# Second layer's chosen tokens: gathered rows and transposes in place of one-hot products

## The chip, the cores and the metric

The kernel runs on one core of a Trainium2 chip, with all weights and inputs in that chip's memory. The metric is the device time of one execution in microseconds, here the median of three runs.

## What is computed

Two layers of a backbone over 512 latent tokens and 256 context tokens of 1024 features, float32. Each layer mixes the tokens (an mLSTM in both directions, a convolution, a Fourier transform, one projection in and one out) and then sends them through 16 experts that choose their own tokens. Only the second part matters here; of the reference it is this (`cap` is 64 for the latents, 32 for the context):

```python
def expert_choice_ffn(xn, w_router, w_gate, w_up, w_down):
    bsz, n, _ = xn.shape
    cap = EC_CAPACITY_FACTOR * n // N_EXPERTS
    aff = jax.nn.softmax(jnp.einsum('bnd,de->bne', xn, w_router).astype(jnp.float32), axis=-1)
    gate, idx = lax.top_k(jnp.swapaxes(aff, 1, 2), cap)
    bidx = jnp.arange(bsz)[:, None, None]
    xs = xn[bidx, idx]
    hid = jax.nn.silu(jnp.einsum('becd,edf->becf', xs, w_gate)) * jnp.einsum('becd,edf->becf', xs, w_up)
    ys = jnp.einsum('becf,efd->becd', hid, w_down) * gate[..., None].astype(xn.dtype)
    return jnp.zeros_like(xn).at[bidx, idx].add(ys)
```

The second layer's experts see the latents alone, since nothing reads the context after it. A final norm over the latents follows.

## The kernel before, in words

**Experts.** They go in pairs, one on each half of the partitions: 8 pairs, each with a gate, an up and a down product of 64 slots by 1024 by 1024 per expert. `wide` (line 1397) does one such product in four quarters; a quarter (q) takes two weight tiles, one of each expert, and issues eight products of 512 columns (line 1410; each is two instructions of the trace). Between the quarters it fills in small work: `pop(turns)` the next pair's tokens, `pop(scat)` the sums into the stream (line 1476), `pop(trans)` the transposes of the hidden values (line 1463). The order on PE is the program's (`manual_schedule`); the other engines' order is set by a scheduler. The loop at line 1646 does gate(p+1), down(p), up(p+1); the last pair's down product, `down_last`, goes by quarters of the columns (line 1618), and the squares for the final norm ride along.

**Weights.** `load_experts` (line 1123) issues the loads on SP's queue in the order in which they are used, one tile of 1 MiB (two blocks of 128 rows of one expert) at a time, into a ring of places `wreg`; a tile that has been used gives its place back. In the second layer the ring has 9 places of its own, filled while the output projection runs, 6 more (`WP`) once the projection's operands are gone, and 1 (`extra`, line 1300): 16. Each load of the ring takes one of eight semaphores in turn.

**The chosen tokens.** After the second norm DVE picks each expert's best tokens by eight rounds of max, index and replace (lines 1234 to 1240), while PE turns the normalised latents into rows by token, `XT`, which ACT copies out of PSUM (lines 1254 and 1255). The places are turned into columns by slot: `GI` and `GP` hold them as floats, `GXu` as whole numbers.

- In the *first layer* the token rows are written to `xrow` in memory by SP (line 1257); `fetch_rows` (line 1332) lets POOL gather a pair's 128 rows by an indirect DMA (line 1337), and `turn` turns them to features by slots with four transposes for each half of the features (line 1363).
- In the *second layer* the rows stay in the buffer. `onehot` (line 1341) spreads a pair's places by one product and compares them on DVE with the token numbers `tcol` (line 1347); `turn` then makes the features by slots with 16 products for each half (line 1360).

In both, DVE and ACT scale and shift the result into `XSp` (lines 1368 and 1370). `fetch_pair(q)` puts a pair's turns on the list, two pairs ahead of their use for the gathers, and the lists are emptied between the quarters. At the stage's start the second layer does the one-hot and the first half's turn before the first gate product, and the second half's turn after that product's first quarter (line 1638):

```python
if last:
    wreg.append(extra)
    load_experts()
fetch_pair(0)
pop(turns, 2 if last else 99)
if not last:
    wreg += wp[4:] + xt_r + [mem.alloc(2048) for _ in range(3)]
    load_experts(gathers)
```

Of the kernel before, what the change touches and what calls it, by code (L numbers as in the profile page):

```python
# [10 lines left out]
OP = mybir.AluOpType  # L11
# [3 lines left out]
D = 1024  # L15
KB = 8
# [6 lines left out]
LAT, CTX = 0, 1  # L23
# [26 lines left out]
ADA1_RATE, AREG, ADA_XTK = 0.3, 19, 1.2  # L50
WORDER = [[KB0 + i for i in range(4)] + p + [QB + i for i in range(4)] + [FB, FB + 1] + [OB + i for i in range(4)]
# [7 lines left out]
class Mem:  # L59
    """Places in the on-chip buffer, in floats of a partition."""  # L60
# [45 lines left out]
class Fill:  # L106
    """Work that is laid between the steps of another: rate is its share of their time."""
# [18 lines left out]
    def run_us(self, us):  # L126
        """about us of it, now"""
        self.credit = us / self.rate * self.rate
        self.run(0.0)
# [25 lines left out]
def build(nc, tc, xT, ctxT, params, w_ada, w_gates, w_in, w_out, w_router, w_e_gate, w_e_up, w_e_down,  # L155
# [6 lines left out]
    def body(A, RB, PS, scr, xrow):  # L162
# [30 lines left out]
        # the float32r operands live in tiles of their own; the place of the largest one is  # L193
        # given to expert weights while no projection runs
# [17 lines left out]
        # ------------------------------------------------------------ constants  # L212
# [7 lines left out]
        _, tcol = new(4)  # L220
# [23 lines left out]
        pool.iota(tcol, pattern=[[128, 4]], base=0, channel_multiplier=1, allow_small_or_imprecise_dtypes=True)  # L244
# [15 lines left out]
        # silu(c), silu(c_ctx) as the two used columns of a 32-column stationary  # L260
# [3 lines left out]
        # ------------------------------------------------------------ adaLN vectors  # L264
        def after(inst, firsts, how=mybir.DependencyClass.Sync):
            """a transfer that takes its turn after others"""
            for f in firsts:
                tc.add_manual_dep(inst.ins, f.ins.name, mybir.DependencyInfo(how, mybir.DependencyReason.DATA),
                                  reason="its turn comes later")

        def ada_round(l, r, ring, bank, eng, firsts=(), some=1):
            ps = B(bank)
            src = w_ada[l].rearrange("(k p) (r g h c) -> r h k p g c", p=128, r=3, g=4, h=2)
            for hf in range(2):
                for k in range(KB):
# [5 lines left out]
                    # some at a time: the array's tiling changes as seldom as it can  # L281
# [14 lines left out]
        def ada_first(ring, bank, bank2, eng, splits):  # L296
            """the first layer's first vectors, by halves of the columns: blocks 0, 1, 4, 5 of the features first"""
# [3 lines left out]
            for hf in range(2):  # L301
# [8 lines left out]
                # the first weights' splits come before  # L310
# [19 lines left out]
        # ------------------------------------------------------------ norms  # L330
        class Sums:
            """sums of squares over the features: four blocks at a time, each on its group of partitions"""
# [16 lines left out]
            def columns(self, out, sb, ps, eng):  # L349
                """1 / root mean square, by token: out [128, chunks]"""  # L350
# [8 lines left out]
        def warm(func, after):  # L359
            """have the function's table in place, after the making of a column, before it is waited for"""  # L360
# [6 lines left out]
        def spread(cols, nch, tmp, ps):  # L367
            """values by token [128, chunks] as rows on every partition"""
# [22 lines left out]
        # ================================================================ a layer  # L391
        for l in range(2):
# [5 lines left out]
            # ---------------- projection weights: loads and splits run ahead of the products  # L398
# [13 lines left out]
            def split_ahead(n):  # L412
                while len(parts) < min(n, len(wseq)):
# [4 lines left out]
                    # the vector engine is the busier one while the convolution runs  # L418
# [13 lines left out]
            # ---------------- first vectors, norm  # L432
# [74 lines left out]
            def gate_rows(some, half):  # L507
                # the gates: four blocks at a time, each on its group of partitions
# [5 lines left out]
            # the first layer's by blocks, while the second half of the vectors comes; the second's  # L514
            # context first, as its sums end before
# [48 lines left out]
            def in_block(label, which):  # L564
# [4 lines left out]
                # the last product leaves the blocks in the order in which the next one's operands take their place  # L569
# [6 lines left out]
            def tview(ap, h, s):  # L576
                """[p, 512] in the head's own token order, seen in raster order [p, r, w]."""
# [9 lines left out]
            # gates: rows 32*(2*dir + head//2) + head%2 (i) and + 2 (f)  # L587
# [41 lines left out]
            def chain():  # L629
                # the gate rows  # L630
# [37 lines left out]
                # the backward scan of the context starts at its last chunk, from nothing  # L668
# [21 lines left out]
                # by tokens: column 4*dir + head  # L690
# [9 lines left out]
                # the running maxima and the states' weights go out, and come back on every partition  # L700
# [3 lines left out]
                # decay, on every partition  # L704
# [17 lines left out]
                # chunk states  # L722
# [40 lines left out]
                def fetch(h):  # L763
                    """a head's rows of both directions on every partition; what a query may not see is masked"""
# [10 lines left out]
                def front(s, h):  # L775
                    """scores of a head, weighted for both directions; queries weighted for the states"""
# [74 lines left out]
                # normalise, transpose, gate; the result takes the gate's place  # L851
# [67 lines left out]
            def convln():  # L919
# [6 lines left out]
                # convolution: LayerNorm, swish  # L926
# [52 lines left out]
            for part in (('v', 'ga') if l == 0 and not GA0 else ('ga', 'v')):  # L979
                if part == 'ga':  # L980
# [16 lines left out]
                    # convolution: the sums take the gates' place  # L997
# [37 lines left out]
            # ---------------- Fourier input, folded: the transform of real numbers  # L1035
# [53 lines left out]
            # ---------------- the output projection; the second norm's sums and the router ride along  # L1089
# [24 lines left out]
            # expert weights run ahead from here on  # L1114
# [8 lines left out]
            def load_experts(firsts=(), most=1000):  # L1123
                while len(wtiles) < min(wtaken[0] + len(wreg), len(wq), most):
                    w, e, i = wq[len(wtiles)]
                    if last and w is w_e_down and e >= E - 2:
                        t = V(wreg[len(wtiles) % len(wreg)], KB, 256)
                        src = w[l, e].rearrange("(k p) f -> p k f", p=128)[:, :, i * 256:i * 256 + 256]
                        # the very last ones in halves: fewer products wait for the end of the transfer
# [632 lines left out]
```

## Time and profile before

| | us |
|---|---|
| runs | 1888.52, 1891.25, 1892.82 |
| median | 1891.25 |
| span of the profiled execution | 1887.4 |
| PE, DVE, ACT, POOL busy in it | 1777.9, 688.1, 452.6, 128.1 |

The profile comes from one execution of its own; only its span is given, from the first to the last instruction, and it lies 1.1 us below the fastest of the three runs. A busy PE is not a PE at its peak, and the shares are means over stages with different limits: the first layer's expert stage lies at about 470 to 1000 us, the second layer's at about 1394 to 1870 us. 518.40 MB are moved in all, most of them the 2 x 192 expert tiles. A row of the stretches gives each engine's busy time with the number of instructions, TensorE's granted clock as a share of full speed, the mean busy share of the 16 DMA engines, and the rate.

### The profile page before, as it was taken

Reading aid. Unit: us, or ns where it says so; the run is one execution under the profiler, and the core shown is the slowest. Engines: PE = TensorE matmul, PEld = TensorE weight load, DVE = VectorE, ACT = ScalarE, POOL = GpSimd, SP = SyncE. Lnnn points to the kernel's source line nnn. Section 1 sums busy time; section 2 is a strip of 40 time slices with the busy share of each in tenths; the row PEclk is TensorE's granted clock in tenths of the full one; section 3 lists DMA queues with packets and bytes.
Section 4 is the critical chain, followed back from the end, with each engine's and each line's share of the span. In section 5 each row is a group of like instructions: output and inputs, shape, how many; then the busy total and the mean of one; then the engine's idle time right before and its main releaser. Section 6 shows DMA issues by size and latency. Waiting matters only on the chain.

```text
span 1887.4 us, 25008 instructions
## 1 busy us (share of the span) xinstructions
PE 1777.9 (94%) x10336; PEld 970.1 (51%) x10336; DVE 688.1 (36%) x1490; ACT 452.6 (24%) x868; POOL 128.1 (7%) x164
## 2 busy tenths in 40 slices
PE   5989999998999999999999998989979999999997
PEld 2667887776333333333333477777744444334433
DVE  4533897424002212122122577956230222111213
ACT  4433454313111001101100363346221101000001
POOL 1022221321000000000000002210000000000000
PEclk8989999998999999999999999999989999999999
DMA  9365344855999999988988113143669999999993
GB/s 340 101 201 194 99 134 148 293 207 218 415 414 384 352 343 345 354 340 325 353 327 320 40 34 95 56 121 101 238 253 416 416 414 414 415 416 416 416 396 120
DMA packets 151377, 518.40 MB, mean 275 GB/s; under 512 B 9696, under 2 KB 29152, under 8 KB 151264
## 3 DMA queue, kind: packets, MB, share of 16 engines
q1 hardware_dynamic: 135392, 456.51, 63.1%
q0 software_dynamic: 15872, 60.30, 9.6%
q8 instruction: 81, 1.33, 0.3%
q14 instruction: 32, 0.26, 0.0%
HBM read 509.96 MB, written 6.82 MB: 274 GB/s over the span
## 4 chain that ended last, share of the span: by engine, by line
PE 76%; DVE 10%; DMA 5%; issue 5%; ACT 2%; SPq 1%; POOL 1%; DVEq 0%; POOLq 0%; ACTq 0%
PE PS L1410 31%; PE PS L485 16%; PE PS L1420 9%; PE PS L1360 3%; PE PS L1476 3%; DVE A L1010 2%; DMA A<-w_e_up 2%; PE PS L279 1%; PE PS L1618 1%; SPq L304 1%; DVE A L1477 1%; PE PS L1497 1%; DMA WP<-w_e_up 1%; PE PS L1463 1%; DMA A<-w_e_down 1%
## 5 line engine op out<-in xcount | busy, mean ns | idle before, releaser
L485 PE MATMUL PS<-RA,RB 128*128 128x512 f32 (+1 forms) x2352 | 513.1, 365 | 19.0 <-ACT A L968 8.0
L1410 PE MATMUL PS<-A 128*64 128x512 f32 x1600 | 427.5, 596 | 5.1 <-DMA A<-w_e_up 4.4
L485 PEld LDWEIGHTS PS<-RA,RB 128*128 128x128 f32 x2352 | 376.9, 193 | 93.8 <-issue 20.8
L1410 PE MATMUL PS<-WP,A 128*64 128x512 f32 x1344 | 370.4, 597 | 1.4 <-DMA WP<-w_e_up 1.4
L1410 PEld LDWEIGHTS PS<-A 128*64 128x64 f32 x1600 | 130.7, 137 | 223.0 <-issue 206.5
L1410 PEld LDWEIGHTS PS<-WP,A 128*64 128x64 f32 x1344 | 111.8, 137 | 180.0 <-issue 173.0
L1477 DVE SCALAR_TENSOR_TENSOR A<-PS,A 128x512 f32<-128x512 f32 x128 | 91.9, 748 | 228.3 <-PE PS L1476 228.3
L1464 ACT ACTIVATE A<-PS 128x512 f32<-128x512 f32 x40 | 23.8, 597 | 354.9 <-PE PS L1463 354.8
L1420 PE MATMUL PS<-WP,A 128*32 128x512 f32 x816 | 108.7, 595 | 0.0
L1010 DVE SCALAR_TENSOR_TENSOR A<-A 128x783 f32<-128x783 f32 (+1 forms) x120 | 107.5, 922 | 0.1
L1368 ACT ACTIVATE A<-PS,A 128x128 f32<-128x128 f32 x80 | 36.4, 457 | 271.4 <-DVE A L1370 271.1
L417 ACT ACTIVATE RB<-A 128x1024 fp32r<-128x1024 f32 x60 | 63.3, 1057 | 128.4 <-PE PS L485 93.2
L1420 PE MATMUL PS<-A 128*32 128x512 f32 x656 | 90.5, 595 | 0.0
L1484 DVE SCALAR_TENSOR_TENSOR RB<-PS,A,RB 128x512 fp32r<-128x512 f32 x30 | 22.5, 751 | 176.1 <-ACT RB L1483 174.3
L1476 PE MATMUL PS<-RB 128*128 128x512 f32 x256 | 82.0, 430 | 0.9 <-DVE A L1477 0.4
L1370 DVE TENSOR_SCALAR A<-PS,A 128x128 f32<-128x128 f32 x80 | 32.6, 410 | 129.3 <-PE PS L1360 62.9
L1501 DVE SCALAR_TENSOR_TENSOR A<-PS,A 128x256 f32<-128x256 f32 x64 | 27.8, 480 | 134.7 <-PE PS L1497 117.6
L1476 PEld LDWEIGHTS PS<-RB 128*128 128x128 f32 x256 | 41.7, 188 | 68.6 <-issue 53.6
L277 POOL DMA_DIRECT2D A<-w_ada x80 | 60.0, 754 | 213.4 <-PE PS L279 120.4
L420 DVE TENSOR_TENSOR RB<-A,RB 128x1024 fp32r<-128x1024 f32 x50 | 60.9, 1222 | 21.5 <-ACT RB L417 21.3
L1360 PE MATMUL PS<-A 128*128 128x128 f32 x512 | 63.0, 283 | 5.0 <-DVE A L1477 4.5
L1360 PEld LDWEIGHTS PS<-A 128*128 128x128 f32 x512 | 60.0, 196 | 12.9 <-DVE A L1477 9.8
(317 smaller groups left out, 1555.0 us busy)
## 6 DMA issues: line engine op xcount, KB each, us to landing
A<-w_e_gate SPq DMA_DIRECT2D x75, 1024.0 KB, 12.1
A<-w_e_up SPq DMA_DIRECT2D x66, 1024.0 KB, 14.2
WP<-w_e_down SPq DMA_DIRECT2D x63, 1024.0 KB, 10.6
A<-w_e_down SPq DMA_DIRECT2D x63, 1024.0 KB, 15.8
WP<-w_e_up SPq DMA_DIRECT2D x62, 1024.0 KB, 12.2
WP<-w_e_gate SPq DMA_DIRECT2D x53, 1024.0 KB, 9.3
A<-w_ada POOLq DMA_DIRECT2D x80, 512.0 KB, 5.2
A<-w_in SPq DMA_DIRECT2D x44, 512.0 KB, 3.6
```

The lines of the kernel that those rows point to most:

```text
L277: after(eng.dma_start(w, src[r, hf, k]), firsts if hf == 0 and k < len(ring.regs) else ())
L417: whi.append(act.activation(h, raw[i], AF.Copy))
L420: wlo.append(eng.tensor_tensor(lo, raw[i], h.bitcast(F32), OP.subtract))
L485: pe.matmul(banks[s][:, :LEN[s]], w[:, k], xin[:, j, k, OFF[s]:OFF[s] + LEN[s]], start=k == k0 and i == 0, stop=k == k1 and i == 2)
L1010: dve.scalar_tensor_tensor(o, i, wcol, o, op0=OP.mult, op1=OP.add)
L1360: pe.matmul(b[:, j], XT[2 + c][:, db * 128:db * 128 + 128], onehots[i][:, c], start=c == 0, stop=c == 3)
L1368: act.activation(dst[:, db], b[:, j], AF.Identity, bias=sh_, scale=sc_)
L1370: dve.tensor_scalar(dst[:, db], b[:, j], sc_, sh_, op0=OP.mult, op1=OP.add)
L1410: pe.matmul(B(o + hf)[64 * e:64 * e + 64, :], lhs(k, e), w[e][:, a, hf * 512:hf * 512 + 512], start=k == 0, stop=k == KB - 1, tile_positio ...
L1420: pe.matmul(B(o + 2)[32 * g:32 * g + 32, :], lhsc(k, e), w[e][:, a, hf * 512:hf * 512 + 512], start=k == 0, stop=k == KB - 1, tile_positio ...
L1476: pe.matmul(b, YS[:, j, db * 128:db * 128 + 128], PM if pm is None else pm, start=j == 0, stop=j == 1)
L1477: dve.scalar_tensor_tensor(X[LAT][:, db], b, MOD[l][:, LAT, 40 + db:41 + db], X[LAT][:, db], op0=OP.mult, op1=OP.add)
```

## The change

In the second layer the token rows are written to `xrow` as in the first, the indices are made whole numbers there too, and POOL gathers each pair's 128 rows; the one-hot code and `tcol` go, and `turn` transposes in both layers. Two places `xg_r` take the gathered rows. The tokens' own rows `xt_r` (two tiles of 1 MiB) become places for weights once they are written and the first gather is done, `extra` goes (`NEXTRA = 0`), so the ring has 9 + 6 + 2 = 17 places. All turns of the first pair now come before the first gate product. In the first layer the order of the places in the ring changes (`xt_r` before `wp[4:]`). The squares of `down_last` take the places of the tokens' features `xs_r` in halves. Comments are dropped as well, which moves later line numbers by one or two and more further down.

```diff
-        _, tcol = new(4)
-        pool.iota(tcol, pattern=[[128, 4]], base=0, channel_multiplier=1, allow_small_or_imprecise_dtypes=True)
...
-            xt_r = [mem.alloc(D) for _ in range(4)] if last else [mem.alloc(2 * D) for _ in range(2)]
+            xt_r = [mem.alloc(2 * D) for _ in range(2)]
...
-                if not last:
-                    sp.dma_start(xrow[s][tc0:tc0 + 128, :], xt)
+                sp.dma_start(xrow[s][tc0:tc0 + 128, :], xt)
...
-            if not last:
-                for r in range(2):
-                    dve.tensor_copy(GXu[64 * r:64 * r + 64, 0:NP], GI[64 * r:64 * r + 64, 1, r:16:2])
+            for r in range(2):
+                dve.tensor_copy(GXu[64 * r:64 * r + 64, 0:NP], GI[64 * r:64 * r + 64, 1, r:16:2])
...
-                extra = mem.alloc(2048, top=True)
+                extra = [mem.alloc(2048, top=True) for _ in range(NEXTRA)]
...
-                ftring = Ring(xtr.regs)
-                xs_r = [mem.alloc(KB * 128) for _ in range(2)]
-                oh_r = [mem.alloc(512)]
...
+            xg_r = [mem.alloc(D) for _ in range(2 if last else 3)]
+            xs_r = [mem.alloc(KB * 128) for _ in range(2)]
+            xgr = Ring(xg_r)
...
-                t = fetched[s, i] = V((0, D, wp[4 + (s == CTX)][2]) if i == 0 else xgr.next(), D)
+                t = fetched[s, i] = V((0, D, wp[4 + (s == CTX)][2]) if i == 0 and not last else xgr.next(), D)
...
-            def onehot(i):
-                def f():
-                    oh = onehots[i] = V(oh_r[0], 4, 128)
-                    b = bank67()[:, 0:128]
-                    pe.matmul(b, GP[:, 1, i:i + 1].to_broadcast([128, 128]), ident, start=True, stop=True)
-                    for c in range(4):
-                        dve.tensor_scalar(oh[:, c], b, tcol[:, c:c + 1], None, op0=OP.is_equal)
-                return f
...
-                        if last:
-                            for c in range(4):
-                                pe.matmul(b[:, j], XT[2 + c][:, db * 128:db * 128 + 128], onehots[i][:, c],
-                                          start=c == 0, stop=c == 3)
-                        else:
-                            pe.transpose(b[:, j], fetched[s, i][:, db * 128:db * 128 + 128], ident)
+                        pe.transpose(b[:, j], fetched[s, i][:, db * 128:db * 128 + 128], ident)
...
-                if last:
-                    turns.append(onehot(q))
-                else:
-                    fetch_rows(LAT, q)
+                fetch_rows(LAT, q)
...
-                ring = Ring(xtr.regs)
+                ring = Ring([(a + i, 512, m) for a, _, m in xs_r for i in (0, 512)])
...
-            if last:
-                wreg.append(extra)
-                load_experts()
             fetch_pair(0)
-            pop(turns, 2 if last else 99)
-            if not last:
-                wreg += wp[4:] + xt_r + [mem.alloc(2048) for _ in range(3)]
-                load_experts(gathers)
+            pop(turns, 99)
+            wreg += xt_r + (extra if last else wp[4:] + [mem.alloc(2048) for _ in range(3)])
+            load_experts(gathers)
```

On PE, at the start of the second layer's expert stage, the order before is this (names: PS is PSUM, A the buffer; L1276 turns the places, L1345 spreads them, L1360 are the one-hot products, L1410 the gate's; `64x512` is one product of a quarter):

```order
L1254 MATMUL PS<-A 128x128 x32
L1276 MATMUL PS<-A 128x64 x2
L1345 MATMUL PS<-A 128x128
L1360 MATMUL PS<-A 128x128 x16
L1410 MATMUL PS<-A 64x512 x8
L1360 MATMUL PS<-A 128x128 x16
L1410 MATMUL PS<-A 64x512 x25
```

and now (L1253, L1274, L1341 and L1385 are the lines of the transposes of the tokens, of the places, of the gathered rows, and of the gate's products):

```order
L1253 MATMUL PS<-A 128x128 x32
L1274 MATMUL PS<-A 128x64 x2
L1341 MATMUL PS<-A 128x128 x8
L1385 MATMUL PS<-A 64x512 x33
```

The spread and the 32 products of the first pair give way to eight transposes, all ahead of the first quarter.

On SP's queue, at the same place, before (WP are the six places that the projection leaves; L1134 issues a weight tile):

```order
L1134 DMA WP_7996<-w_e_up 128x2x1024
L1134 DMA WP_7997<-w_e_up 128x2x1024
L1134 DMA A<-w_e_gate 128x2x1024 x8
L1134 DMA A<-w_e_down 128x2x1024
L1134 DMA WP_7992<-w_e_down 128x2x1024
```

and now (L1133 issues a weight tile, L1255 writes 128 token rows):

```order
L1133 DMA WP_7995<-w_e_up 128x2x1024
L1133 DMA WP_7996<-w_e_up 128x2x1024
L1255 DMA xrow_67<-A 128x1024 x4
L1133 DMA A<-w_e_up 128x2x1024
L1133 DMA A<-w_e_gate 128x2x1024 x8
L1133 DMA A<-w_e_down 128x2x1024 x2
L1133 DMA WP_7991<-w_e_down 128x2x1024
```

The four writes stand behind the six loads, and the last up tile of the first pair, which was loaded during the output projection before, now stands behind the writes; it and the first of the eight gate tiles go to the places of the token rows.

On POOL's queue the second layer ended with a memset; now the eight gathers follow it (the last but one row is the end of the program):

```order
L770 AFFINE_SELECT A<-A 128x512 x2
L1196 MEMSET A 128x192
L1331 DMA A<-xrow_67,A 128x1024 x8
L1729 UNCONDITIONAL_BRANCH
L1729 ISA
```

Nothing else stands between the gathers there.

## Rows read from the trace of the kernel before

**Rows 1.** The page: busy time, and DMA share and rate in 40 slices.
```profile
PE 1777.9 (94%) x10336; PEld 970.1 (51%) x10336; DVE 688.1 (36%) x1490; ACT 452.6 (24%) x868; POOL 128.1 (7%) x164
...
DMA  9365344855999999988988113143669999999993
GB/s 340 101 201 194 99 134 148 293 207 218 415 414 384 352 343 345 354 340 325 353 327 320 40 34 95 56 121 101 238 253 416 416 414 414 415 416 416 416 396 120
```

**Rows 2.** Stretches of the second expert stage: PE, PEld, DVE, ACT, POOL, clock, DMA.
```profile
1410.00:1502.22 92.22, 91.47 (x478) 40.76 (x476) 15.86 (x31) 10.39 (x18) 0.00 (x0) 1.00 1.03 416
1502.22:1559.08 56.86, 56.11 (x284) 24.28 (x286) 11.73 (x21) 5.60 (x10) 0.00 (x0) 1.00 1.03 415
...
1673.00:1830.00 157.00, 149.50 (x704) 61.30 (x702) 27.74 (x48) 14.19 (x25) 0.00 (x0) 1.00 1.03 414
1830.00:1850.00 20.00, 18.40 (x82) 9.33 (x78) 5.50 (x8) 3.05 (x5) 0.00 (x0) 1.00 1.06 342
```

**Rows 3.** The chain that ended last: start, us, what.
```profile
1501.63 0.59 PE PS L1463 x4
1502.22 20.75 PE PS L1410 x96
1522.97 0.42 PE PS L1345 x2
...
1528.47 3.84 PE PS L1360 x32
...
1559.08 20.75 PE PS L1410 x96
...
1673.90 18.55 DMA A<-w_e_up
...
1810.48 19.02 DMA A<-w_e_up
```

**Rows 4.** SP's queue in order of time: start, us, line, issues.
```profile
1694.45 15.00 SPq L1134 DMA_DIRECT2D WP<-w_e_gate  x6
```

**Rows 5.** The first layer's transposes, line 1363: duration min/median/max in ns, first and last start.
```profile
L1363 PE MATMUL PS<-A x80: 272/273/331, 496.6 to 944.6; 128*128 128x128 f32 x80
```

**Rows 6.** Stretches around the opening of the second expert stage.
```profile
1370.00:1380.00 10.00, 6.22 (x39) 5.77 (x38) 7.61 (x33) 6.85 (x12) 0.00 (x0) 0.83 1.03 413
1380.00:1385.00 5.00, 0.67 (x2) 0.31 (x2) 4.39 (x19) 0.83 (x3) 0.00 (x0) 0.93 0.65 260
1385.00:1390.00 5.00, 3.01 (x12) 2.72 (x13) 3.32 (x14) 0.00 (x0) 0.00 (x0) 0.50 0.00 0
...
1395.00:1400.00 5.00, 5.00 (x36) 3.26 (x33) 0.00 (x0) 0.11 (x1) 0.00 (x0) 1.00 0.27 72
1400.00:1410.00 10.00, 10.00 (x53) 4.03 (x53) 0.82 (x2) 0.92 (x2) 0.00 (x0) 1.00 0.80 315
```

**Rows 7.** The opening in order of time: start, us, engine, what.
```profile
1366.07 3.26 SPq L1134 DMA_DIRECT2D WP<-w_e_up  x6
...
1377.05 3.17 ACT L1255 ACTIVATE A<-PS,A 128x512 f32<-128x512 f32 x5 [0.17 <-PE PS L1254]
...
1385.89 0.17 DVE L1292 SCALAR_TENSOR_TENSOR A<-A 128x16 f32<-128x16 f32 x1
...
1393.73 3.65 PE L1410 MATMUL PS<-A 128*64 128x512 f32 x16 [0.51 <-DVE A L1370]
```

**Rows 8.** First layer: landing times of lines 1337 and 1257, and PE's opening.
```profile
DMA to landing us min/median/max: 4.4/5.8/7.6
...
DMA to landing us min/median/max: 2.6/2.7/4.8
...
465.80 1.67 PE L1363 MATMUL PS<-A,WP 128*128 128x128 f32 x8 [0.81 <-DMA WP<-xrow,A]
...
470.72 4.76 PE L1410 MATMUL PS<-WP,A 128*64 128x512 f32 x16
```

**Rows 9.** A stretch in which PE waits for weights.
```profile
1810.00:1820.00 10.00, 7.38 (x34) 2.29 (x32) 1.50 (x2) 1.37 (x2) 0.00 (x0) 1.00 1.03 420
```

More of the change, by code (lines that the diff above doesn't have):

```diff
@@ L50 @@
 ADA1_RATE, AREG, ADA_XTK = 0.3, 19, 1.2
+NEXTRA = 0
 WORDER = [[KB0 + i for i in range(4)] + p + [QB + i for i in range(4)] + [FB, FB + 1] + [OB + i for i in range(4)]
@@ L1320, in body @@
                 _, PM2 = new(512, mem=memb)
-                ftring = Ring(xtr.regs)
-                xs_r = [mem.alloc(KB * 128) for _ in range(2)]
-                oh_r = [mem.alloc(512)]
             XSp, XSq = {}, {}
+            xg_r = [mem.alloc(D) for _ in range(2 if last else 3)]
+            xs_r = [mem.alloc(KB * 128) for _ in range(2)]
+            xgr = Ring(xg_r)
             if not last:
-                xg_r = [mem.alloc(D) for _ in range(3)]
-                xs_r = [mem.alloc(KB * 128) for _ in range(2)]
-                xgr = Ring(xg_r)
                 xc_r = [mem.alloc(KB * 128) for _ in range(2)]
@@ L1339, in fetch_rows @@
                 after(gathers[-1], before, NOSYNC)
-            def onehot(i):
-                def f():
-                    oh = onehots[i] = V(oh_r[0], 4, 128)
-                    b = bank67()[:, 0:128]
-                    pe.matmul(b, GP[:, 1, i:i + 1].to_broadcast([128, 128]), ident, start=True, stop=True)
-                    for c in range(4):
-                        dve.tensor_scalar(oh[:, c], b, tcol[:, c:c + 1], None, op0=OP.is_equal)
-                return f
-            onehots = {}
             def turn(s, i, hf):
```

## The prediction

> **What bounds the kernel now.** I read the page's forty slices first [rows 1]. PE is busy 94% of the span, which invites the thought that every product taken off it is time won. The last two rows say where that fails: in the first layer's expert stage (slices 12 to 21) the transfers run at 320 to 384 GB/s under a full PE, but in the second layer's (slices 30 to 37) they stand at 414 to 416 GB/s without a dip. I then cut that stage into stretches [rows 2]: from 1410 to 1830 us the DMA engines' share is 1.03 and the rate 414 to 416 GB/s in every stretch. So both PE and the transfers are nearly full, and the question is which one ends last. The chain of waits [rows 3] answers. The same 20.75 us piece of gate products starts at 1502.22 and at 1559.08: PE needs 56.85 us for a pair of experts as long as it waits for nothing. A pair's weights are 24 tiles of 1 MiB, 25.17 MB, and at 415 GB/s that is 60.6 us. PE is the faster by 3.8 us a pair; it lives on the 16 tiles that were loaded ahead, and by 1673.90 they are used up: from there the chain runs through transfers of 18.55 and 19.02 us, until the last tile of the last up product lands at 1829.5. SP shows the same pace: six loads issued in 15.00 us, 2.5 us each [rows 4], which is one tile at 415 GB/s. After 1829.5 nothing but PE and what follows it counts; the remaining transfers (narrower rows, 342 GB/s [rows 2]) end near 1850 and the span at 1887.4. So the end is set by the moment at which the last up tile lands, and that by two things: when the transfers start to run without a pause, and how many bytes have to go through.
>
> **The change, part by part.** All sums are against the profiled execution's span of 1887.4 us; the median of the runs, 1891.25, is 3.85 above it, and I carry that over.
>
> *PE's turns.* Per pair the chain loses two pieces of 3.84 us (16 one-hot products each) and the 0.42 us that spreads the places [rows 3]. In their place come 8 transposes; one of the first layer's lasts 273 ns [rows 5], and four of the same kind go through in 0.59 us pipelined (the chain's piece at 1501.63 [rows 3]), so 1.2 us. PE's pair falls by 8.10 - 1.2 = 6.9 us to about 50 us. This is worth nothing, because the transfers already need 60.6; it only brings forward the moment at which PE waits for them. What covers it is the stream of weights; if that had room, it would be worth 8 x 6.9 = 55 us (a rival below).
>
> *New bytes.* Four writes of the normalised tokens, 0.524 MB each, and eight gathers of 128 rows, also 0.524 MB each. While the stream is full each gather costs 0.524 MB / 415 GB/s = 1.26 us. Bounds: nothing, if it falls into an idle stretch; 1.26 us otherwise, and twice that, 2.5 us, if its rows moved at half the rate, of which no row shows a sign. I take 1.26 for those in the full stream. [...]
>
> *The opening.* Before, the transfers are idle from 1383 to 1397 and half idle to 1405 [rows 6]: all 16 tiles lie there, and SP can issue only when the first quarter of the first gate product, begun at 1393.73 and 3.65 us long [rows 7], gives two tiles back. The 10 us to 1410 move 3.15 MB and the 5 us before them 0.36 [rows 6], 3.35 tiles: at 1410 there are 19.35 tiles. Now the same for the change, step by step. Only 15 tiles are loaded ahead (the 16th place lies in the token rows). The six loads issued from 1366.07 [rows 7] fill the engines until 1383.1 (1.30 MB are left at 1380 [rows 6]). ACT has the last token rows ready at 1380.2 [rows 7], so the four writes stand behind those loads on SP's queue: 2.10 MB, 5.05 us, to 1388.2, and about 1 us until they count as landed (a single one takes 2.6 us for 1.26 us of data at the best [rows 8]): 1389.2. The places are ready on DVE by 1386.5 (1386.06 [rows 7] and the two new casts, 0.35 us), so the writes come last. Gather 0 then starts at 1389.5 and takes 4.4 us, the shortest of the first layer's, which had idle engines too [rows 8]: 1393.9. Eight transposes, 1.67 us as there [rows 8], then the first gate quarter, from 1395.7. PE has stood idle for longer than before, so I give this quarter the 4.76 us it took in the first layer in the same place [rows 8], not 3.65: to 1400.5. The two tiles that wait for gather 0 are issued at 1394 and move from 1395.4; gather 1 goes ahead of them into the idle stretch, and gather 2, free after the first transposes, beside them. The engines are then full to 1401.7 and go on with the two tiles that the first quarter gives back. At 1410 that makes 17 + 8.1 us / 2.525 us = 20.2 tiles: 0.85 tile or 2.1 us ahead of before. What is queued behind the waiting loads on SP is only the tiles whose places come free after 1400.5, so this wait holds up nothing.
>
> *The rest.* Five gathers remain inside the full stream: 5 x 1.26 = 6.3 us. POOL has no other work beside the gathers, DVE loses four compares per pair, and neither is waited for. The 17th tile is worth what the opening counts for it and no more, since a deeper store does not speed a full stream. In the first layer two loads change places; PE is the bound there at 340 GB/s [rows 1], so this costs nothing. The ring for the last squares moves to tiles that the last up product has left; nothing waits. The tail after the last up tile stays as it is.
>
> Sum: -2.1 + 6.3 = +4.2 us, 1891.6 of span, 1895.5 us beside the median.
>
> **Where these lines are moved to** is seen in the change's section: the four writes stand between the six loads and the rest on SP, and PE has the eight transposes in one piece before the first gate product.
>
> **The rivals.**
> *PE is the bound after all* (the other side: faster). For it speaks PE's 94% and that PE waits in 1673 to 1830 for only 7.5 of 157 us [rows 2]. It decides if the engines can carry more than 415 GB/s once PE releases tiles sooner; at 420, the most that a 10 us stretch here shows [rows 9], the 420 us of the stage lose 1.2% or 5 us, about what the gathers cost; full use would bring 55 us: 1836 to 1887. Against it: over the 157 us to 1830, in which PE at last wants tiles sooner than they come, the mean is 414 [rows 2]. Chance 0.07.
> *The opening hides more* (no change). If the writes did not queue behind the loads, gather 0 would start after DVE's casts, at 1386.8, and land at 1391.2, 2.7 us sooner; with the first quarter at full clock another 1.1. Then +0.4 to +1.5: 1892 to 1893. Against it stands the single queue. Chance 0.18.
> *The gather comes late.* The longest landing in the first layer was 7.6 us [rows 8]; 3.2 us more in the opening pass on whole, and gathers at less than the full rate add up to 6: +7 to +13, 1898 to 1904. Chance 0.08.
> *The clock falls.* PE will now wait in every pair, some 12 us of 60.6 + 1.3. In the opening its granted clock went to 0.50 after idling [rows 6]; a quarter then takes 4.76 in place of 3.65 us. If each of a pair's twelve quarters paid these 1.1 us, PE would need 63.2 us a pair and be the bound, 1.3 us above the stream: 8 x 1.3 = 10 us more, 1906; if only the tail began so, 1897. [...] Against it: with PE idle 26% of the time from 1810 to 1820 the clock stayed at 1.00 [rows 9], since the waits are short. Chance 0.05.
> My forecast's own case (+2 to +7) keeps 0.62.
>
> **How the numbers follow.** About 0.2%, 3.8 us, is what a measurement tells from no change: 1887.5 to 1895.0 is the same. Faster is the first rival, 0.07. The same takes the second rival and a third of the forecast's case, 0.18 + 0.20 = 0.38. Slower is the rest, 0.55. The range takes the forecast's case (1893.3 to 1898.3), the no-change rival and the nearer half of the late gather and the clock; with 1.5 us for the median's own scatter at both ends that is 1890 to 1902. The forecast's own range is 1893 to 1898.5.
>
> **What would show it.** Right: 415 GB/s from about 1396 on without a gap; PE's products wait for weight transfers from the third pair on, and in sum for far more than before; the last up tile lands near 1834; the first gate product starts near 1395.7, held by gather 0, and that by the last write. Wrong: a stream above 420 GB/s or pairs shorter than 60 us (PE was the bound); a first gate product before 1393.5, or gathers whose landing leaves the weights' rate as it was (the price of bytes is wrong); a granted clock below 1.00 in the middle of the stage.

## The result, and the profile after

The change is slower: 1903.02 us median (1901.80 to 1906.33, 4 runs) against 1890.53 (1888.52 to 1892.82, 4 runs) for the kernel before, a ratio of 1.0070 with a 95% interval of 1.0055 to 1.0084. That is +12.5 us where +4.2 were forecast; the sign is right, the size is outside the range. The profiled execution of the change has a span of 1902.4 us (its own time 1904.15), 15.0 above the one of before.

The page's row of busy times and its rows of DMA share and rate in 40 slices, to be read against [rows 1]:

```profile
PE 1744.2 (92%) x9872; PEld 918.4 (48%) x9872; DVE 679.5 (36%) x1460; ACT 452.5 (24%) x868; POOL 135.3 (7%) x171
...
DMA  9266343856999999998997112234689999999993
GB/s 337 100 205 194 108 145 122 304 195 246 410 409 379 353 353 335 357 343 324 344 341 264 34 56 83 67 103 131 261 340 409 409 409 409 409 410 409 409 392 125
```

PE lost 33.7 us of work and the kernel became longer. The row to look at is the last: in the second expert stage (slices 31 to 38) the rate is 409 or 410 GB/s, where it was 414 to 416. It is also 410 and 409 in the eleventh and twelfth slices, which lie in the *first* layer, where it was 415 and 414. The diff does nothing to the loads there but swap two of them. So the rate of the weights' transfers itself changed, and in the first layer the new gathers cannot be the reason.

The stretches that answer to [rows 2] and [rows 6] (same columns: PE, PEld, DVE, ACT, POOL, clock, DMA share, GB/s):

```profile
1380.00:1385.00 5.00, 0.96 (x8) 0.56 (x6) 4.86 (x21) 1.98 (x4) 0.00 (x0) 1.00 1.00 372
1385.00:1390.00 5.00, 0.70 (x2) 0.35 (x2) 3.91 (x18) 0.62 (x2) 0.00 (x0) 0.52 0.98 400
1390.00:1395.00 5.00, 0.00 (x0) 0.00 (x0) 0.00 (x0) 0.00 (x0) 2.02 (x2) 0.50 0.18 30
1395.00:1400.00 5.00, 2.93 (x12) 2.01 (x14) 1.15 (x4) 0.96 (x3) 0.71 (x1) 0.50 0.77 235
1400.00:1410.00 10.00, 10.00 (x44) 3.09 (x42) 0.40 (x1) 0.76 (x2) 0.23 (x1) 0.89 0.99 379
...
1500.00:1600.00 100.00, 85.85 (x355) 29.02 (x356) 18.47 (x30) 8.80 (x16) 1.88 (x2) 1.00 1.03 409
1600.00:1700.00 100.00, 85.91 (x350) 28.00 (x348) 13.27 (x22) 7.98 (x14) 0.94 (x1) 1.00 1.03 409
1700.00:1800.00 100.00, 89.40 (x371) 32.61 (x373) 21.16 (x34) 9.40 (x17) 0.00 (x0) 1.00 1.03 409
```

Three things stand there. The writes fill the engines to 1390 (400 GB/s) as the prediction had it, and then there is a hole to about 1396. In the stage the DMA share is 1.03 in every stretch, and PE, busy 86 to 89%, waits. And the rate is 409 from 1700 to 1800 as well, after the last gather (POOL has nothing there).

The chain that ended last, in order of time (start, us, what), from the opening and from the stage, for [rows 3]:

```profile
1382.01 9.76 DMA xrow<-A
1391.77 0.02 issue
...
1392.62 4.32 DMA A<-xrow,A
...
1397.07 1.94 PE PS L1341 x8
...
1474.10 22.20 DMA A<-w_e_down
...
1496.36 20.39 DMA A<-w_e_up
...
1516.81 21.70 DMA WP<-w_e_gate
...
1844.16 4.03 PE PS L1385 x15
```

In the opening: the last write lands at 1391.77, POOL issues gather 0 at 1392.62, it takes 4.32, eight transposes take 1.94. From 1474 on the chain goes mostly through transfers of 18 to 22 us, one after another; before, it went through such transfers (18.55 and 19.02 us) only from 1673.9 on.

To compare traces whose stages begin at different moments, I count each from the eight products that make the router's logits, the first work behind the output projection's sums (line 1203 before). Then the span falls into three: to the first gate product, from there to the chain's last piece of the last up product, and the rest.

| trace | router products | first gate | last up piece | end | opening | stage | tail | sum |
|---|---|---|---|---|---|---|---|---|
| before | 1369.5 | 1393.7 | 1829.6 | 1887.4 | 24.2 | 435.8 | 57.9 | 517.9 |
| the change | 1370.8 | 1398.9 | 1844.2 | 1902.4 | 28.1 | 445.2 | 58.2 | 531.6 |
| e1_b_shift | 1368.4 | 1394.0 | 1837.2 | 1896.3 | 25.6 | 443.2 | 59.1 | 527.9 |
| e2_a_gap | 1370.9 | 1399.1 | 1835.4 | 1894.3 | 28.2 | 436.4 | 58.9 | 523.4 |
| e3_b_less_pe | 1371.4 | 1396.8 | 1831.9 | 1890.6 | 25.4 | 435.1 | 58.7 | 519.2 |
| e4_b_align | 1376.0 | 1401.5 | 1837.7 | 1896.8 | 25.5 | 436.2 | 59.1 | 520.8 |
| e5_b_256 | 1372.8 | 1397.6 | 1829.5 | 1888.2 | 24.8 | 431.9 | 58.7 | 515.4 |
| e6_a_256 | 1374.1 | 1402.1 | 1836.7 | 1894.4 | 28.0 | 434.6 | 57.7 | 520.3 |
| e7_a_write_first | 1375.4 | 1400.0 | 1836.7 | 1895.6 | 24.6 | 436.7 | 58.9 | 520.2 |
| e8_a_two_gathers | 1379.7 | 1407.7 | 1839.3 | 1897.5 | 28.0 | 431.6 | 58.2 | 517.8 |
| e9_a_256_write_first | 1368.2 | 1393.4 | 1826.1 | 1884.4 | 25.2 | 432.7 | 58.3 | 516.2 |
| e10_b_256_less_pe | 1373.6 | 1397.7 | 1828.3 | 1887.1 | 24.1 | 430.6 | 58.8 | 513.5 |

The router's products move by 11 us between executions, for reasons ahead of the stage; the opening and the tail of kernels that do the same there agree within 1.5 us. The change lost 13.7 us behind the router's products: 3.9 in the opening, 9.4 in the stage, 0.3 in the tail.

### The profile page after: what moved, and what is told of

The parts are those of the page before. It is cut to its first block, busy times and chain, and to the rows that moved or that the text cites. A ratio compares the mean times of both kernels' runs of the same rounds, so it can differ in the third digit from the quotient of the medians.

```text
span 1902.4 us, 24067 instructions
## 1 busy us (share of the span) xinstructions
PE 1744.2 (92%) x9872; PEld 918.4 (48%) x9872; DVE 679.5 (36%) x1460; ACT 452.5 (24%) x868; POOL 135.3 (7%) x171
## 3 DMA queue, kind: packets, MB, share of 16 engines
q8 instruction: 77, 1.26, 0.3%
## 4 chain that ended last, share of the span: by engine, by line
PE 64%; DMA 18%; DVE 9%; issue 5%; ACT 2%; SPq 1%; POOL 1%; DVEq 0%; POOLq 0%; ACTq 0%
PE PS L1385 23%; PE PS L484 16%; PE PS L1395 9%; DMA A<-w_e_down 4%; DMA A<-w_e_up 3%; DMA WP<-w_e_up 3%; PE PS L1451 2%; DVE A L1009 2%; DMA WP<-w_e_gate 2%; DMA WP<-w_e_down 2%; PE PS L278 2%; PE PS L1593 1%; PE PS L1341 1%; DMA A<-w_e_gate 1%; PE PS L1472 1%
## 5 line engine op out<-in xcount | busy, mean ns | idle before, releaser
L1385 PE MATMUL PS<-A 128*64 128x512 f32 x1608 | 452.7, 599 | 31.3 <-DMA A<-w_e_down 25.3
L1385 PE MATMUL PS<-WP,A 128*64 128x512 f32 x1336 | 387.8, 600 | 15.2 <-DMA WP<-w_e_down 10.1
L1385 PEld LDWEIGHTS PS<-A 128*64 128x64 f32 x1608 | 135.8, 137 | 263.6 <-issue 198.7
L1385 PEld LDWEIGHTS PS<-WP,A 128*64 128x64 f32 x1336 | 115.6, 137 | 202.5 <-issue 168.8
L1395 PE MATMUL PS<-WP,A 128*32 128x512 f32 x816 | 123.9, 595 | 0.0
L1395 PE MATMUL PS<-A 128*32 128x512 f32 x656 | 105.7, 595 | 0.0
L1331 POOL DMA_INDIRECT A<-xrow,A x18 | 17.0, 947 | 607.8 <-PE PS L1341 572.3
L1458 ACT ACTIVATE RB<-PS,A 128x512 fp32r<-128x512 f32 x30 | 20.6, 688 | 155.8 <-PE PS L1385 145.0
```

Source lines behind the costliest of these rows:

```text
L1385: pe.matmul(B(o + hf)[64 * e:64 * e + 64, :], lhs(k, e), w[e][:, a, hf * 512:hf * 512 + 512], start=k == 0, stop=k == KB - 1, tile_positio ...
L1395: pe.matmul(B(o + 2)[32 * g:32 * g + 32, :], lhsc(k, e), w[e][:, a, hf * 512:hf * 512 + 512], start=k == 0, stop=k == KB - 1, tile_positio ...
```

## The experiments

Ten kernels ran, on three chips. The kernel before ran beside them: its median was 1891.72 us for e1 to e4, 1896.86 for e5 to e8, 1892.08 for e9 and e10. So the ratios are to be compared, not the times.

**Where the rate went: `tcol`.** The change deletes the token numbers `tcol`. They took 64 bytes near the start of the buffer A, and every place allocated after them moved down by 64. In the kernel before, as built, seven of the nine places of the ring in A begin 256 bytes past a multiple of 512 and two 384 past one, the six of WP 480, and `extra` 160. In the change nine of the eleven places in A begin 192 bytes past a multiple of 512 and two 320, WP's 480 still. So seven of sixteen places lie on multiples of 256 bytes before, and none of seventeen in the change. The theory: a weight tile whose lines begin off some boundary moves more slowly. The rival: the gathers, or the writes, slow the stream.

*e1_b_shift*: the kernel before, with nothing but the 64 bytes taken out of that place.

```diff
-        _, tcol = new(4)
+        _, tcol = new(4, top=True)
```

> The kernel before, with the four columns of token numbers (tcol) at the other end of the buffer, so that every other place lies 64 bytes lower, as in the change; nothing else is altered. Theory (the place of the tiles sets the rate of the loads): the 9 of 16 weight tiles whose packets took 159 ns take 163.6 ns, the stream of the second expert stage falls from 415 to 409 GB/s, and its 165 tiles after 1410 us cost 0.041 us more each: 6.7 us slower than before, about 1897. Rival (the gathers slow the stream, or that chip was slower): 415 GB/s and no change, 1890.5.

*e2_a_gap*: the change, with 64 unused bytes put back.

```diff
         _, iot = new(TL)
+        _, gap = new(4)
         _, eps = new(1)
```

> The changed kernel with an unused place of 16 numbers where tcol stood, so that the places lie as they did before; nothing else is altered. Theory of the places: 11 of 17 weight tiles go back to 159 ns a packet, the stream rises from 409 to about 416 GB/s, and 165 tiles at 0.045 us less give 7.5 us back: about 1895.5. Rival (gathers slow the stream): 409 GB/s and no change against the changed kernel, 1903.

Measured: e1 1897.81 us, ratio to before 1.0036 (1.0023 to 1.0048); e2 1896.15 us, 1.0027 (1.0015 to 1.0039). A stretch of e1 and one of e2, columns as above:

```profile
1500.00:1600.00 100.00, 98.49 (x506) 43.58 (x504) 18.81 (x35) 10.31 (x19) 0.00 (x0) 1.00 1.03 409
```

```profile
1500.00:1600.00 100.00, 88.31 (x369) 31.93 (x366) 19.27 (x31) 8.80 (x16) 1.87 (x2) 1.00 1.03 418
```

The kernel before without any gather falls to 409 GB/s when its places move by 64 bytes; the change with all its gathers rises to 418 when they move back. The gathers are acquitted. In the stage the 64 bytes cost e1 7.4 us (443.2 against 435.8) and the change 8.8 (445.2 against 436.4); by the ratios it is 6.8 and 8.1, near the expected 6.7 and 7.5.

The mixture can be seen directly. This is the rate from 1500 to 1800 us in 40 slices of 7.5 us, three tiles each, of the kernel before:

```profile
GB/s 419 413 410 413 418 421 417 407 410 418 421 418 412 410 412 422 421 415 408 411 422 418 421 410 409 418 421 421 412 411 413 418 418 419 408 411 417 422 418 409
```

and of the change:

```profile
GB/s 410 407 410 407 410 410 407 410 409 411 409 407 409 410 410 407 409 410 409 409 408 410 411 410 409 409 407 410 410 409 409 407 410 411 407 411 410 409 410 407
```

Before, the rate swings between 421 and 408 as the ring goes round; after, it is flat at the lower level. The times of single packets of 4 KB in the traces say the same: before, nine tiles of every sixteen take 159.0 ns a packet and seven 163.5; in the change and in e1 all take 163.6. A tile of 1.049 MB takes 2.49 us at the one and 2.56 at the other.

**Which boundary.** If seven tiles of sixteen move at the lower rate before, the places that cause it can be brought to the higher.

*e4_b_align*: the kernel before, WP and `extra` on multiples of 128 bytes.

```diff
-    TOTAL = 53000 - RA_N - RB_N
+    TOTAL = 53000 - RA_N - RB_N - 8
...
+            p.tile([128, 24], F32, name="WGAP")
```

> The kernel before, with the seven of its 16 weight places whose packets took 163.6 ns (the six WP and the extra one) moved by 32 bytes to multiples of 128 bytes; nothing else is altered. Theory of the places: all packets take 159.0 ns, the stream of the second expert stage rises from 415 to about 421 GB/s, and 165 tiles at 0.032 us less give 5 us: about 1885.5, faster than both kernels. Rival (the place does not matter): 1890.5.

Measured: 1894.18 us, ratio 1.0012 (1.0003 to 1.0021). A miss: no gain, and this stretch still reads

```profile
1500.00:1600.00 100.00, 98.87 (x496) 41.46 (x492) 18.46 (x34) 10.28 (x18) 0.00 (x0) 1.00 1.03 416
```

So 128 bytes are not the boundary (WP now began at 384 past a multiple of 512). Its stage was as long as before (436.2), and the tiles of its WP places landed 2.56 us apart, as those of WP before. The traced execution, the longest of its eleven, reached the router's products late (1376.0); what made the median 0.1% longer is not shown. The edit also moved the float32r operands by 32 bytes; whether that did it was not tried.

*e5_b_256*: the kernel before, WP and `extra` on multiples of 256 bytes, nothing else moved.

```diff
+            p.tile([128, 56], F32, name="WGAP")
...
-                extra = mem.alloc(2048, top=True)
+                extra = (mem.alloc(2096, top=True)[0] + 8, 2048, mem)
```

> The kernel before, with the six WP places and the seventeenth place (extra) moved to multiples of 256 bytes; the float32r tile RB stays where it was. Theory (what counts is whether a weight tile's place begins at a multiple of 256 bytes): 7 of 16 places turn fast, the rate of the second expert stage rises from 415 to 420 to 423 GB/s, and the time falls by 4 to 6 us, to about 1886.5. First rival (any other difference between WP and A makes these seven slow, not the address): 415 GB/s and the time of before, 1891.7. Second rival (PE is the bound above 415 GB/s): the rate rises only while places are free, and the time falls by less than 2 us.

(The place called the seventeenth there is `extra`, the sixteenth.) Measured: ratio 0.9974 (0.9963 to 0.9985), 1892.27 us on this chip, 4.9 us below before by the ratio; by the two traces' sums it is 2.5 (517.9 to 515.4), 3.9 of gain in the stage. The rate from 1500 to 1800 us in 40 slices is now

```profile
GB/s 421 417 421 423 421 418 420 418 418 422 420 419 419 421 418 422 421 421 418 421 423 418 421 421 421 417 423 421 420 419 421 421 418 421 421 421 418 422 418 419
```

flat at the upper level, and the packets take 159.0 ns throughout. The swing is gone: the boundary is 256 bytes. This version is faster than both kernels, by 0.3 and 1.0% in the ratios.

One thing limits this. Two of the ring's places in A still begin 128 bytes past a multiple of 256, as in the kernel before, so not all places of e5 are aligned (nor of e6, e9 and e10, whose expectations say so). By the trace of e5 their tiles land 2.56 and 2.55 us after the tile ahead of them (medians in the stage), much as tiles off the boundary do in the other runs, but the three tiles behind them land after 2.44 to 2.46, and nothing of it is left in the rate. Before, nine places off the boundary follow one another in the ring (WP, `extra` and these two), and seven tiles of sixteen have slow packets; in e2 they stand as six and two, and only four to five of seventeen have. So the loss of about the first two in a row is made up for; by what is not shown.

*e6_a_256*: the change with the gap of e2 and the same WGAP, so fifteen of its seventeen places begin on multiples of 256 (the expectation says all of sixteen).

> The changed kernel with the 64 bytes put back (as in e2_a_gap) and the six WP places at multiples of 256 bytes, so that all sixteen places are aligned. Theory of the address: the rate goes from 417.5 to 420 to 423 GB/s, the time 3.5 to 5.5 us below e2_a_gap, about 1891.5, no slower than the kernel before. Rival (not the address): 417.5 GB/s and 1896.

Measured: ratio 1.0006 (0.9993 to 1.0019), 420 GB/s in its stretches from 1500 to 1800, a stage of 434.6 us against 436.4 of e2. By the ratios the gain over e2 is 4 us (1.0027 to 1.0006), within the expected 3.5 to 5.5 though the intervals together leave it uncertain by 3; the traces show 3.1 (520.3 against 523.4).

**PE's saving.** *e3_b_less_pe*: the kernel before, with the one-hot products of all pairs but the first cut to one block of tokens of four, which takes three quarters of two pieces of 3.84 us, 5.76 us a pair, off PE and adds no byte.

```diff
-                            for c in range(4):
+                            nc_ = 4 if i == 0 else 1
+                            for c in range(nc_):
```

> The kernel before, in which the one-hot products of all pairs but the first use one of the four blocks of token rows, so that most chosen tokens are left out: 24 of a pair's 32 products go, some 5.8 us of TensorE a pair, and no transfer is added or moved. Theory (the weights' stream sets the end): TensorE waits for weights instead, and the time stays within 1 us of the kernel before, 1890.5. Rival (TensorE is the bound): 7 x 5.8 = 41 us faster, 1850.

Measured: 1892.09 us, ratio 0.9999 (0.9988 to 1.0009). Two stretches of it:

```profile
1500.00:1600.00 100.00, 91.85 (x402) 33.29 (x398) 21.52 (x39) 8.80 (x16) 0.00 (x0) 1.00 1.03 415
1600.00:1700.00 100.00, 87.20 (x377) 30.23 (x376) 15.35 (x27) 9.37 (x16) 0.00 (x0) 1.00 1.03 415
```

PE does less and waits more; 415 GB/s, not a GB more. 40 us of PE's work (7 x 5.76) taken off an engine that is busy 94% bought nothing.

*e10_b_256_less_pe*: the same cut on e5, where the stream is faster and PE's 57 us a pair are nearer to its 59.9.

> The kernel before with all places aligned (e5_b_256), and of the one-hot products of all pairs but the first only one block of four, as in e3_b_less_pe (so most of those chosen tokens are left out): PE loses 5.76 us a pair where the stream runs at 420 GB/s, 59.9 us a pair, against some 57 of PE. Theory (the stream still sets the end, as the last up tile in e5 was waited for): within 1.5 us of e5_b_256, ratio to the kernel before 0.9966 to 0.9982, some 515 us from the router's products to the end. Rival (at 420 GB/s PE holds the stream back by releasing places late): 3 us or more below e5_b_256, ratio 0.9958 or less.

Measured: ratio 0.9973 (0.9961 to 0.9984), as e5's; the trace's stage 430.6 against 431.9, its sum 513.5 against 515.4, 1.9 us less where like kernels differ by up to 1.5 us in the opening alone. Still the stream sets the end.

**The opening.** *e7_a_write_first*: e2, with the last two of the six WP loads issued behind the four writes.

```diff
-            wreg += wp if last else wp[:4]
+            wreg += wp[:4]
...
             mem.free([list(tr.values()), rc_r])
+            if last:
+                wreg += wp[4:]
+                load_experts()
```

> The changed kernel with the 64 bytes put back, and the last two of the six WP loads issued behind the four writes of the token rows. Theory (the opening is set by the writes that queue behind the loads): the last write lands near 1386, gather 0 then waits only for its places on DVE, starts near 1389 and lands near 1393.5 in place of 1397; the first gate product starts some 3.5 us sooner and the time falls by 2.5 to 4 us against e2_a_gap, to about 1893. Rival (the opening's delay is made up for later, or the held-back loads leave a gap of their own): within 1 us of e2_a_gap, 1896.

Measured: ratio 1.0013 (1.0002 to 1.0025). Its opening in order of time (start, us, engine, what; in brackets the idle time before and what ended it):

```profile
1371.98 2.12 SPq L1134 DMA_DIRECT2D WP<-w_e_up  x4
1382.82 4.07 SPq L1256 DMA_DIRECT2D xrow<-A  x4
1386.93 1.36 SPq L1134 DMA_DIRECT2D WP<-w_e_up  x2
1392.55 0.34 DVE L1296 CAST A<-A 64x8 uint32<-64x8 f32 x2
...
1393.64 1.10 POOL L1335 DMA_INDIRECT A<-xrow,A  x1 [26.75 <-DVE A L1307]
1398.13 1.94 PE L1345 MATMUL PS<-A 128*128 128x128 f32 x8 [6.75 <-DMA A<-xrow,A]
```

In the change POOL waited for the last write:

```profile
1387.99 0.35 DVE L1292 CAST A<-A 64x8 uint32<-64x8 f32 x2
...
1392.62 1.03 POOL L1331 DMA_INDIRECT A<-xrow,A  x1 [30.29 <-DMA xrow<-A]
```

Now it waits for DVE, whose casts write the places that the gather reads (the row names L1307, the copy right behind them, which the gather does not read). The opening falls from 28.2 to 24.6 us, and the kernel's sum from 523.4 to 520.2; by the ratios the gain is 2.6 us, with intervals that overlap. (The times in the expectation were those of e2; here all lies 4.5 us later, as the router's products do.) The place on SP's queue is what made the opening late, and a later start of the stream is not won back in it.

**The gathers' price.** *e8_a_two_gathers*: e2 with the gathers of pairs 2 to 7 left out.

```diff
+                if last and i > 1:
+                    return
                 before = gathers[-1:]
```

> The changed kernel with the 64 bytes put back, and of the second layer's eight gathers only those of the first two pairs; the later pairs turn and multiply the same rows again, so the tokens of experts 4 to 15 are left out. Five gathers of 0.524 MB fall into the full stream, a sixth (pair 2's) into its beginning. Theory (a gather in the full stream costs its bytes at the stream's rate, 1.26 us each): 6.3 to 7.6 us less than e2_a_gap, about 1889. Rival one (gathers are hidden beside the weights): 1896. Rival two (rows by indirect transfer move at half the rate): 12 us less or more, 1884.

Measured: ratio 0.9988 (0.9978 to 0.9997), against e2's 1.0027 a gain of 7.4 us, by intervals some 3 either way; by the traces' sums 5.6 (523.4 to 517.8), 4.8 of it in the stage. For the five that fall into the full stream that is 1.0 to 1.5 each: the forecast's 1.26 stands, and neither "hidden" nor "half rate" does.

**What the change is worth when its two other costs are mended.** *e9_a_256_write_first*: e6 and e7 together.

> The changed kernel with all sixteen places at multiples of 256 bytes (as in e6_a_256) and two of the six WP loads issued behind the four writes (as in e7_a_write_first): its two mendable costs taken away at once, the bytes of the gathers left. Counted from the router's eight products (the first work that depends on the end of the output projection) to the end of the span, the kernel before took 517.9 us, e6 520.3, and the reordering was worth 3.2 us between e2 and e7. Theory (address, opening and gathers add up): 517.1 us from there, ratio to the kernel before 0.997 to 1.000, and no better than e5_b_256 (515.4 us, 0.9974), since the gathers' 5 to 6 us stay. Rival (with address and opening mended, PE's saving begins to count): 512 us or less from there, clearly faster than e5.

Measured: ratio 0.9988 (0.9977 to 1.0000), sum 516.2 us (517.1 expected). The casts and the first gate product of it:

```profile
1385.19 0.34 DVE L1298 CAST A<-A 64x8 uint32<-64x8 f32 x2
...
1393.42 9.09 PE L1391 MATMUL PS<-A 128*64 128x512 f32 x34
```

So mended the change is no slower than the kernel before, but not better than the aligned kernel before (0.9974). The two intervals overlap a little, so the order is not shown beyond doubt; it is the one that the theory gives, since e9 moves twelve times 0.524 MB more. The distance is smaller than the gathers' 5 to 6 us, though: 0.8 us by the traces, 2.7 by the ratios. The change's place more in the ring, one tile or 2.5 us, may be part of it; no run took that place alone away. The rival (512 us or less) falls.

## Why the prediction was wrong in size

Point by point:

- **"That is set by the moment at which the last up tile lands ... when the transfers start to run without a pause, and how many bytes have to go through"**: right, with a third term that it left out: at what rate. From 1474 on the chain of the change goes mostly through transfers.
- **PE's saving "is worth nothing"**: right. e3 and e10 take 40 us of PE's work away and gain 0.0% by the ratios. The rival "PE is the bound" falls; its condition, that the engines carry more than 415 GB/s if PE releases sooner, is not met in e3.
- **The step that failed: the 415 GB/s as a constant.** The sum took the rate of before for the stage of the change. Every edit that adds or removes bytes was costed, but what the deletion of `tcol` does to the places of everything behind it was not: the diff's line was counted as nothing. At 409 GB/s for 415 the 420 us of the stage are 1.5% longer: 6.2 us. (Against e2 it is 8.8 us, since with the 64 bytes in place the change would have had more fast tiles than the kernel before.) The rows shown hinted at it: a stretch of before reads 420 [rows 9] while the mean was 414 to 416 [rows 2]. The prediction used the 420 only as a bound for a rival; it was the rate of the fast tiles.
- **The opening, "-2.1 us"**: wrong sign, by its size. The mechanism was as told (writes behind the six loads, then gather 0, then eight transposes, then the first gate product at half clock: 0.50 granted up to 1400), but three pieces were short. In times of the kernel before (1.35 us earlier, by SP's issue of the six loads), the last write landed at 1390.4, not 1389.2; POOL issued gather 0 0.85 us behind it, not 0.3; the transposes took 1.94, not 1.67. The gather itself, 4.32 us, was as forecast (4.4). The first gate product came 3.9 us later than before's, where 2.0 were forecast. In tiles: the stretches above move 5.12 MB from 1390 to 1410, three gathers of 0.524 are in that, and the other 3.55 MB are 3.4 tiles on top of 15; 1.4 us later, at the moment that corresponds to 1410, it is 18.9 tiles. The forecast had 20.2, before had 19.35. So the opening lost 0.45 tile, 1.2 us, where 2.1 were to be gained: 3.3 us. (The forecast's own sum also has a slip: from 1401.7 to 1410 are 8.3 us, not 8.1, 0.1 tile.)
- **The gathers, "+6.3 us"**: right in size (e8: 5.6 by the traces, 7.4 by the ratios).
- **"A deeper store does not speed a full stream"**: right for the rate, which is 420 GB/s in e6 with seventeen places as in e5 with sixteen, but the two new places give e2 nine of seventeen on multiples of 256, against seven of sixteen before, and leave four to five slow tiles of seventeen against seven of sixteen. That lifts its rate from 415 to 417 or 418 and gives back some 2.5 us (0.6% of 420). That is why e2, the change without its accident, lands at +5.1 us by its ratio, near the forecast's +4.2, with two errors of opposite sign in it.
- **The sum** with the two mended terms is 4.2 + 6.2 + 3.3 = 13.7 us; the traces show 13.7, the medians 12.5.
- **The clock**: as forecast. It is 0.50 in the opening, from 1390 to 1400, where PE stood idle for 5.17 us up to 1386.13 and for 10.24 us up to 1397.07, and 1.00 in the stage though PE waits 11 to 14% of it, at most 2.6 us at a time. The prediction put the 1.00 of before, from 1810 to 1820, down to short waits; the longest there is 1.4 us. That the clock held because they are short is its author's estimate; no run tried it. The rival falls.
- **"The opening hides more"** needed writes that do not queue behind the loads. e7 puts them ahead of two of the six, and gains 3.6 us of opening.

What the forecast called the case "gather comes late" (0.08) had nearly the measured number (+7 to +13) by another mechanism: the gathers did not come late, the weights did.

## What to carry over

Where a stream of transfers sets the end, its rate is a term of the sum like its bytes: look at it slice by slice, and ask of a rate that swings (between 421 and 408 GB/s in the kernel before) which tiles move at its lower level. An edit that only deletes a small constant moves every later place in a hand-managed buffer, and so can change the speed of transfers that it does not touch (64 bytes took the rate of before, 415 GB/s, to e1's 409); compare the start of the streamed places modulo 256 bytes, the boundary of these runs (e4 416 GB/s, e5 420), before and after, and pin them. In this stage work taken off an engine that is busy 94% was worth nothing while the stream beside it was full (e3: 40 us of PE's work, ratio 0.9999), and bytes added to that stream cost about their full time (e8: 1.0 to 1.5 us a gather, 1.26 by its bytes).

## What the runs showed of the hardware

A stream of 1 MiB tiles from memory into the buffer, in lines of 4 KB, ran at 420 to 421 GB/s in e5 and e6, where all places but two began on multiples of 256 bytes in the buffer, and at 409 in the change and e1, where none did: 2.8% less, with 159.0 and 163.6 ns a packet. It made no difference how far off they were: tiles at 64, 192 and 224 bytes past a multiple of 256 in the change, 160 before and 128 in e4 all landed some 2.56 us after the tile ahead of them. With two such places by themselves (128 bytes past, in e5 and e6) the stream ran at the upper rate, and e5's packets took 159.0 ns.

The boundary is that of these runs: e4's multiples of 128 bytes gained nothing (416 GB/s, ratio 1.0012), e5's multiples of 256 brought the upper rate (420 GB/s, ratio 0.9974), and the faster places of the kernel before lay 256 bytes past a multiple of 512. What moved is the place in the buffer that is written; why the rate depends on it is not shown.
